# A gated layer on one core: the values pass placed ahead of the pass of seven products, with the weight sums stored in between

## The chip, the cores and the metric

The kernel runs on one core of one Trainium2 chip. The metric is device time in microseconds (us) of one execution; the runs of a kernel are given as a median with the lowest and highest.

## What is computed

The reference is one layer of a hybrid encoder on x (4096 positions, 1024 features): RMS norm, one input projection, then three groups side by side (dilated attention, a gating unit, attention into 256 memory tokens), each times SiLU of its gate, one output projection, a residual and a last RMS norm. The change touches the gating unit alone:

```python
uv = jax.nn.gelu(sg_uv)
u, vv = jnp.split(uv, 2, axis=-1)
vv = layer_norm(vv, sg_ln_g[layer], sg_ln_b[layer])
vv = vv.reshape(B, S // SG_CHUNK, SG_CHUNK, N_SG_GROUPS, SG_GROUP_DIM)
mixed = jnp.einsum('gpq,bcqge->bcpge', sg_w[layer], vv)
mixed = mixed + jnp.transpose(sg_b[layer])[None, None, :, :, None]
y_sg = (u * mixed.reshape(B, S, SG_WIDTH)) * jax.nn.silu(g_sg)
```

sg_uv and g_sg are 1024 and 512 columns of h @ w_in. So three blocks of 512 columns are projected for it: u, vv and the gate.

## The kernel before

All matmuls work on pairs of numbers: every operand is split into a high part (ACT copies it to fp32r, tiles xh, wh) and a low part (VectorE subtracts the high part, tiles xl, wl), and each product is three matmuls (high x high, high x low, low x high). A 128x512 block with 1024 input features is 8 x 3 = 24 matmuls.

The work runs in passes. **Pass A** (lines 242 to 318) projects q, k and the attention's values over eight tiles T of 512 positions. **Pass U** (lines 393 to 467) computes u and the gate together: as a 2x2 block product with seven instead of eight sub-products (Winograd's form). For that, split_parts (lines 338 to 391) forms seven weight blocks B11, T2, B22, T1, T3, B21, T4 of four 128x512 tiles each, in three rounds at the last T of pass A; it reads 40 raw blocks of 256 KB. Pass U has 16 rounds r of 256 positions. prep(r) loads x (line 404), scales it on POOL (line 406), forms the sums S1 to S4 on POOL (lines 418, 419, 422, 426) and splits seven x blocks (lines 414, 415). A round is seven product() calls of 12 matmuls (line 434) into three accumulators b1, b2, b3, with additions by VectorE in between (lines 447 to 460), and GELU and SiLU on ACT (lines 461 to 464); the result GELU(u) * SiLU(gate) is stored to DRAM as ug (line 467). **Pass B** (lines 470 to 525), the values pass, projects vv with Wvv over eight T, four blocks j each; GELU (line 498), layer norm (lines 500 to 506) and a split (lines 507, 508) follow on ACT, VectorE and POOL; then 24 matmuls of 128x256 (line 520, tile pm) form the weight sums, and VectorE adds the bias and multiplies by u, which was loaded back from ug (lines 492, 524). **Pass C** starts with the memory tokens: projections with Wmv (line 595) and Wmk (line 608), rsb (line 331), weights Wqm (line 587).

Buffers that all passes share lie in pool px: five raw tiles, ten xh and ten xl. Weight tiles lie in slots 0 (px), 1, 2 (pool pw) and 3 (pool pz); slots 0 to 2 hold eight tiles each, so a weight takes the slot when the one before is used up. Inside a pass every pass has its own pool, which lies over that of the pass before it.

The order of the instructions on each engine is made by a planner, which goes by its own estimates of cost and takes what is ready, earlier lines first. From the last T of pass B to line 616 in pass C the order on TensorE, ACT and VectorE is that of the program (ORDERED, line 52). The order of the passes is in build:

```python
with tc.tile_pool(name="pz", bufs=2, reuse_waits="tile") as b.pz:
    b.pass_a()
    b.pass_u()
b.order = ExitStack()
b.pass_b()
gates = b.pass_g(env)
for _ in b.pass_c(env):
    next(gates)
```

Of the kernel before, what the change touches and what calls it, by code (L numbers as in the profile page):

```python
# [18 lines left out]
S = 4096  # L19
# [35 lines left out]
class Builder:  # L55
    def __init__(self, ctx, tc, a):
# [38 lines left out]
        dt("ug", [S, 512])  # L95
# [146 lines left out]
    def pass_a(self):  # L242
        nc, tc, a = self.nc, self.tc, self.a
        with tc.tile_pool(name="pa", bufs=2, reuse_waits="tile") as p, \
# [26 lines left out]
            for T in range(NT):  # L271
# [23 lines left out]
                if T == NT - 1:  # L295
                    values(T, X, rs)
                    self.split_parts(0)
                for W, done, dh, dl in ((Wq, pq, self.qH, self.qL), (Wk, pk, self.kH, self.kL)):
                    for cb in range(4):
# [5 lines left out]
                        if T == NT - 1 and cb == 3:  # L305
                            self.split_parts(1 if W is Wq else 2)
# [28 lines left out]

    PAIR = 2048, 3072

    def split_parts(self, rnd):


        nc = self.nc
        if rnd == 0:
            self.WS = {}
        g_ = self.g_in

        def raw(i, j, kt):
            t = self.px.tile([P, 512], F32, name="raw", tag="raw", bufs=5)
            nc.sync.dma_start(t, self.a["w_in"][(4 * i + kt) * P:(4 * i + kt + 1) * P, self.PAIR[j]:self.PAIR[j] + 512])
            return t

        def put(name, slot, src, g, kt):
            pool = (self.px, self.pw, self.pw, self.pz)[slot]
            n = 4 if slot == 3 else 8
            h = pool.tile([P, 512], F32R, name="wh", tag="wh%d" % slot, bufs=n)
            lo = pool.tile([P, 512], F32R, name="wl", tag="wl%d" % slot, bufs=n)
            self.WS[name, kt] = h, lo
            if g is None:
                nc.scalar.copy(h, src)
                nc.vector.tensor_sub(lo, src, f(h))
            else:  # L360
                nc.scalar.activation(h, src, AF.Copy, scale=g)
                nc.vector.scalar_tensor_tensor(lo, src, g, f(h), ALU.mult, ALU.subtract)

        def tmp():
            return self.pz.tile([P, 512], F32, name="wt", tag="wt", bufs=2)

        for kt in range(4):
            g1, g2 = g_[:, kt:kt + 1], g_[:, kt + 4:kt + 5]
            b11, b12, b22 = raw(0, 0, kt), raw(0, 1, kt), raw(1, 1, kt)
            if rnd == 0:  # L370
                put("B11", 0, b11, g1, kt)
            if rnd != 1:
                d, t2 = tmp(), tmp()
                nc.gpsimd.tensor_sub(d, b12, b11)
                nc.scalar.activation(d, d, AF.Copy, scale=g1)
                nc.vector.scalar_tensor_tensor(t2, b22, g2, d, ALU.mult, ALU.subtract)
            if rnd == 0:
                put("T2", 0, t2, None, kt)
                put("B22", 3, b22, g2, kt)
            elif rnd == 1:  # L380
                d, t3 = tmp(), tmp()
                nc.gpsimd.tensor_sub(d, b12, b11)
                put("T1", 1, d, g1, kt)
                nc.scalar.activation(b12, b12, AF.Copy, scale=g1)
                nc.vector.scalar_tensor_tensor(t3, b22, g2, b12, ALU.mult, ALU.subtract)
                put("T3", 1, t3, None, kt)
            else:
                b21 = raw(1, 0, kt)
                put("B21", 2, b21, g2, kt)
                nc.vector.scalar_tensor_tensor(t2, b21, g2, t2, ALU.mult, ALU.subtract)  # L390
                put("T4", 2, t2, None, kt)

    def pass_u(self):

        nc, tc, a = self.nc, self.tc, self.a
        with tc.tile_pool(name="pu", bufs=1, reuse_waits="tile") as p, tc.tile_pool(name="ppu", bufs=2, space=PSUM, reuse_waits="tile") as pp:
            rsb = {}

# [1037 lines left out]
```

## Time and profile before

| what | value |
|---|---|
| median of 3 runs | 3135.18 us (3132.35 to 3145.68) |
| the profiled execution's own time | 3133.94 us |
| its span, first to last instruction | 3132.2 us |
| mean granted TensorE clock | 0.983 of full speed |
| TensorE busy | 2985.4 us, 95% |
| first and last store of ug (pass U's rounds) | 643.9 and 934.5 us |

Times in the rows count from the start of the span. PE is TensorE's matmuls, PEld its weight loads, DVE is VectorE, POOL is GpSimd, SPq the queue of DMA issues of SyncE. The granted clock is 1.00 at 2.4 GHz and 0.50 at 1.2 GHz; a value in between is a mean over the stretch. An arrow in brackets names what ended the idle time ahead of an instruction. A matmul's given length overlaps with the next one's.

### The profile page before, as it was taken

Reading aid. Unit: us, or ns where it says so; the run is one execution under the profiler, and the core shown is the slowest. Engines: PE = TensorE matmul, PEld = TensorE weight load, DVE = VectorE, ACT = ScalarE, POOL = GpSimd, SP = SyncE. Lnnn points to the kernel's source line nnn. Section 1 sums busy time; section 2 is a strip of 40 time slices with the busy share of each in tenths; the row PEclk is TensorE's granted clock in tenths of the full one; section 3 lists DMA queues with packets and bytes.
Section 4 is the critical chain, followed back from the end, with each engine's and each line's share of the span. In section 5 each row is a group of like instructions: output and inputs, shape, how many; then the busy total and the mean of one; then the engine's idle time right before and its main releaser. Section 6 shows DMA issues by size and latency. Waiting matters only on the chain. (4 is left out here: it accounts for less than half of the span.)

```text
span 3132.2 us, 44554 instructions
## 1 busy us (share of the span) xinstructions
PE 2985.4 (95%) x15658; PEld 2496.4 (80%) x15658; DVE 1626.9 (52%) x3889; ACT 1343.0 (43%) x2675; POOL 555.6 (18%) x800
## 2 busy tenths in 40 slices
PE   9989999599999989999999989999999998999999
PEld 7777888478887878888888868888888876888887
DVE  4222323676657776555553335656665564443443
ACT  5213112345553446555553346677767652111111
POOL 1102113465511100000000011222212211121120
PEclk9999999799999999999999999999999999999999
DMA  8558545522235553112117557777877468777773
GB/s 285 185 162 255 174 135 171 192 88 88 88 109 172 174 177 113 48 55 73 48 53 218 167 126 153 150 150 161 164 162 152 105 174 225 212 192 203 208 190 100
DMA packets 373895, 474.43 MB, mean 151 GB/s; under 512 B 155331, under 2 KB 247838, under 8 KB 364454
## 3 DMA queue, kind: packets, MB, share of 16 engines
q1 hardware_dynamic: 355656, 429.20, 49.3%
q0 software_dynamic: 17440, 41.33, 5.3%
q8 instruction: 124, 2.03, 0.3%
q10 hardware_dynamic: 576, 1.05, 0.1%
q14 instruction: 99, 0.81, 0.1%
HBM read 332.83 MB, written 138.60 MB: 151 GB/s over the span
## 5 line engine op out<-in xcount | busy, mean ns | idle before, releaser
L201 PE MATMUL acc<-xl,wh 128*128 128x512 f32 x1192 | 470.9, 395 | 13.3 <-DVE xl L187 13.2
L200 PE MATMUL acc<-xh,wh 128*128 128x512 f32 x1192 | 472.4, 397 | 8.1 <-ACT xh L186 8.1
L202 PE MATMUL acc<-xh,wl 128*128 128x512 f32 x1192 | 470.5, 395 | 0.0
L880 ACT ACTIVATE p<-ring,negm 128x256 f32<-128x256 f32 (+1 forms) x768 | 330.7, 478 | 167.5 <-DVE negm L867 167.5
L791 DVE CUSTOM_DVE_ANT_0 ring<-s,tab 128x256 f32<-128x256 f32 (+1 forms) x768 | 272.1, 392 | 109.9 <-PE s L786 87.6
L201 PEld LDWEIGHTS acc<-xl,wh 128*128 128x128 f32 x1192 | 226.0, 190 | 66.1 <-DVE xl L187 17.8
L200 PEld LDWEIGHTS acc<-xh,wh 128*128 128x128 f32 x1192 | 225.8, 189 | 59.6 <-ACT xh L186 10.3
L202 PEld LDWEIGHTS acc<-xh,wl 128*128 128x128 f32 x1192 | 226.4, 190 | 47.3
L933 PE MATMUL o<-ph,vt 128*65 128x256 f32 (+1 forms) x1280 | 246.5, 340 | 9.3 <-DMA vt<-v 9.3
L949 DVE COPY oacc<-o 65x512 f32<-65x512 f32 x192 | 132.1, 688 | 203.2 <-PE o L933 140.7
L786 PE MATMUL s<-khh,qs 128*128 128x256 f32 (+1 forms) x768 | 228.4, 322 | 0.0
L186 ACT CAST xh<-raw 128x512 fp32r<-128x512 f32 x256 | 151.7, 620 | 172.1 <-DMA raw<-in_xT_s 96.6
L933 PEld LDWEIGHTS o<-ph,vt 128*65 128x65 f32 x1280 | 166.9, 140 | 70.8 <-issue 11.9
L434 PE MATMUL b<-wh,xh 128*128 128x512 f32 x448 | 178.2, 398 | 34.8 <-ACT xh L414 27.8
L187 DVE TENSOR_TENSOR xl<-raw,xh 128x512 fp32r<-128x512 f32 x256 | 167.7, 686 | 79.3 <-ACT xh L186 77.8
L1257 PE MATMUL acc<-w,aa 128*128 128x512 f32 x768 | 191.4, 399 | 15.3 <-ACT aa L1242 9.9
L200 PE MATMUL acc<-wh,xh 128*128 128x512 f32 x512 | 199.7, 390 | 0.0
L202 PE MATMUL acc<-wh,xl 128*128 128x512 f32 x512 | 199.6, 390 | 0.0
L201 PE MATMUL acc<-wl,xh 128*128 128x512 f32 x512 | 199.5, 390 | 0.0
L786 PE MATMUL s<-kll,qs 128*128 128x256 f32 (+1 forms) x768 | 198.8, 283 | 0.0
L1257 PEld LDWEIGHTS acc<-w,aa 128*128 128x128 f32 x768 | 146.0, 191 | 50.4 <-ACT aa L1242 10.4
L434 PE MATMUL b<-wh,xl 128*128 128x512 f32 x448 | 177.6, 396 | 3.4 <-DVE xl L415 3.4
(277 smaller groups left out, 5817.3 us busy)
## 6 DMA issues: line engine op xcount, KB each, us to landing
raw<-in_xT_s SPq DMA_DIRECT2D x256, 256.0 KB
raw<-in_w_in SPq DMA_DIRECT2D x96, 256.0 KB
og<-oD SPq DMA_DIRECT2D x16, 1536.0 KB
w3k<-wD SPq DMA_DIRECT2D x32, 768.0 KB
oD<-oacc POOLq DMA_DIRECT2D x46, 512.0 KB, 4.7
xn<-in_x_s SPq DMA_DIRECT2D x32, 512.0 KB
v<-t POOLq DMA_DIRECT2D x128, 128.0 KB, 5.5
xr<-in_xT_s SPq DMA_DIRECT2D x16, 1024.0 KB
```

The costliest lines, as they stand in the source:

```text
L186: nc.scalar.copy(h[:, :n], raw[:, :n])
L187: nc.vector.tensor_sub(lo[:, :n], raw[:, :n], f(h[:, :n]))
L200: nc.tensor.matmul(out, lh, rh, start=i == 0, stop=False)
L201: nc.tensor.matmul(out, lh, rl, start=False, stop=False)
L202: nc.tensor.matmul(out, ll, rh, start=False, stop=i == n - 1)
L434: nc.tensor.matmul(ps, l[:, k, :], w, start=first and k + i == 0, stop=k == 3 and i == 2, skip_group_check=True)
L786: nc.tensor.matmul(ps[:, b1, :B["n"]], q, kv, start=i == 0, stop=i == 1)
L791: self.last_dve = nc.vector.tensor_tensor_reduce(out=ring[:, bi, :n], in0=ps[:, b1, :n], in1=e["tab"][:, c, 64 * B["o"]:64 * B["o"] + n], ...
L880: nc.scalar.activation(out, in_, AF.Exp, bias=e["negm"][:, bi:bi + 1], scale=1.0)
L933: nc.tensor.matmul(o[:, o0:o1], vt[:, t, :], pT[:, c0:c1], start=t == 0, stop=t == 4, skip_group_check=True)
L949: nc.vector.tensor_copy(dst, o)
L1257: nc.tensor.matmul(ps, l, w, start=a, stop=o, skip_group_check=True)
```

## The change

The passes run in the order A, B, U, C. Pass B stores the weight sums with their bias, in a DRAM tensor mix, and pass U multiplies by them. In detail: (1) split_parts is gone; at the last T of pass A, Wvv is loaded into slot 0. (2) Pass B's function mix evicts the sums with ACT (Identity with a bias) instead of VectorE and stores y; it is called after the first projection of the next T, and for the last T after the loop. (3) split_early forms B11, T1, T2, T3, B22 at T = 2 to 5 of pass B (slots 1, 2, 3), 12 raw blocks; split_late forms B21 and T4 (slot 0) after the last projection of pass B, 16 raw blocks. w_block and put_w, not shown, are raw and put of split_parts. (4) split_x replaces prep; for round 0 it is called inside pass B and uses four raw tiles; sums are formed in place; the scaling is in two halves. (5) A round of pass U also loads 256 rows of mix (y) and multiplies them on POOL. (6) The stretch in program order begins with the last round of pass U, and the loads of the memory tokens, Wmv and Wmk move there. pass_u's product() is the same as before and is left out.

```diff
-        dt("ug", [S, 512])
+        dt("mix", [S, 512])
...
-                    self.split_parts(0)
+                    self.Wvv = self.load_w(0, self.w_in(2560), self.g_in)
...
-                        if T == NT - 1 and cb == 3:
-                            self.split_parts(1 if W is Wq else 2)
...
-            raw = p.tile([P, 8, P], F32, name="sgraw")
+            raw = p.tile([P, 8, P], F32, name="sgraw", tag="y")
...
+            def mix(T, vvh, vvl):
+                y = p.tile([P, 4, 512], F32, name="y", tag="y")
+                for g2 in range(4):
+                    pm = pp.tile([P, 2, 256], F32, name="pm", bufs=4)
+                    for g in (2 * g2, 2 * g2 + 1):
+                        cs = slice(g * 64, (g + 1) * 64)
+                        self.mm3(pm[:, g % 2, :], [((sw[0][:, g, :], sw[1][:, g, :]), (vvh[:, :, cs], vvl[:, :, cs]))])
+                    for g in (2 * g2, 2 * g2 + 1):
+                        cs = slice(g * 64, (g + 1) * 64)
+                        pv = pm[:, g % 2, :].rearrange("p (c e) -> p c e", e=64)
+                        nc.scalar.activation(y[:, :, cs], pv, AF.Identity, bias=sgb[:, g:g + 1])
+                nc.sync.dma_start(self.mix[T * TT:(T + 1) * TT, :].rearrange("(j p) c -> p j c", p=P), y)
+            vv = None
             for T in range(NT):
-                if T == NT - 1:
-                    self.order.enter_context(tc.manual_schedule(engines=ORDERED))
                 X = self.load_x(a["xT_s"][:, T * TT:(T + 1) * TT])
-                vvh = p.tile([P, 4, 512], F32R, name="vvh")
-                vvl = p.tile([P, 4, 512], F32R, name="vvl")
-                u = p.tile([P, 4, 512], F32, name="u", tag="u", bufs=2)
-                nc.sync.dma_start(u, self.ug[T * TT:(T + 1) * TT, :].rearrange("(j p) c -> p j c", p=P))
                 for j in range(4):
                     rs = rsn[:, 4 * T + j:4 * T + j + 1]
-                    t = p.tile([P, 512], F32, name="t", tag="t1", bufs=3)
+                    self.proj_N(ps, self.Wvv, X, j)
+                    if j == 0:
+                        if T > 0:
+                            mix(T - 1, *vv)
+                        vv = [p.tile([P, 4, 512], F32R, name=n) for n in ("vvh", "vvl")]
+                    if j == 3 and T == NT - 1:
+                        X = self.split_x(0, None)
+                        for kt in range(4):
+                            self.split_late(kt)
+                    t = p.tile([P, 512], F32, name="t", tag="t1", bufs=2)
...
+                    nc.scalar.copy(vv[0][:, j, :], t)
+                    nc.vector.tensor_sub(vv[1][:, j, :], t, f(vv[0][:, j, :]))
+                if 2 <= T < 6:
+                    self.split_early(T - 2)
+            mix(NT - 1, *vv)
+            self.X0 = X
...
+    def split_early(self, kt):
+        nc = self.nc
+        if kt == 0:
+            self.WS = {}
+        g1, g2 = self.g_in[:, kt:kt + 1], self.g_in[:, kt + 4:kt + 5]
+        b11, b12, b22 = self.w_block(0, 0, kt), self.w_block(0, 1, kt), self.w_block(1, 1, kt)
+        self.put_w("B11", 1, b11, g1, kt)
+        nc.gpsimd.tensor_sub(b11, b12, b11)
+        self.put_w("T1", 2, b11, g1, kt)
+        nc.scalar.activation(b11, b11, AF.Copy, scale=g1)
+        nc.vector.scalar_tensor_tensor(b11, b22, g2, b11, ALU.mult, ALU.subtract)
+        self.put_w("T2", 1, b11, None, kt)
+        nc.scalar.activation(b12, b12, AF.Copy, scale=g1)
+        nc.vector.scalar_tensor_tensor(b12, b22, g2, b12, ALU.mult, ALU.subtract)
+        self.put_w("T3", 2, b12, None, kt)
+        self.put_w("B22", 3, b22, g2, kt)
+    def split_late(self, kt):
+        nc = self.nc
+        g1, g2 = self.g_in[:, kt:kt + 1], self.g_in[:, kt + 4:kt + 5]
+        b21, b11, b12, b22 = self.w_block(1, 0, kt), self.w_block(0, 0, kt), self.w_block(0, 1, kt), self.w_block(1, 1, kt)
+        self.put_w("B21", 0, b21, g2, kt)
+        nc.gpsimd.tensor_sub(b11, b12, b11)
+        nc.scalar.activation(b11, b11, AF.Copy, scale=g1)
+        nc.vector.scalar_tensor_tensor(b11, b22, g2, b11, ALU.mult, ALU.subtract)
+        nc.vector.scalar_tensor_tensor(b11, b21, g2, b11, ALU.mult, ALU.subtract)
+        self.put_w("T4", 0, b11, None, kt)
+    def split_x(self, r, p):
+        nc, a = self.nc, self.a
+        if r % 2 == 0:
+            self.rsb = self.pz.tile([P, TT], F32, name="rsb", bufs=1)
+            nc.sync.dma_start(self.rsb, self.rD[:, r * NI:r * NI + TT].broadcast_to([P, TT]))
+        rs = self.rsb[:, r % 2 * NI:(r % 2 + 1) * NI].rearrange("p (o t) -> p o t", o=1)
+        src = a["xT_s"][:, r * NI:(r + 1) * NI].rearrange("(k p) t -> p k t", p=P)
+        if p is None:
+            x = [self.px.tile([P, 512], F32, name="raw", tag="raw", bufs=5).rearrange("p (k t) -> p k t", k=2) for _ in range(4)]
+            for i in range(4):
+                nc.sync.dma_start(x[i], src[:, 2 * i:2 * i + 2])
+            A = [[x[2 * j + e][:, :, P * i:P * (i + 1)] for e in range(2)] for i in range(2) for j in range(2)]
+        else:
+            t = p.tile([P, KT, NI], F32, name="xr", bufs=2)
+            nc.sync.dma_start(t, src)
+            x = [t[:, :4], t[:, 4:]]
+            A = [[t[:, 4 * j:4 * j + 4, P * i:P * (i + 1)]] for i in range(2) for j in range(2)]
+        for t in x:
+            nc.gpsimd.tensor_mul(t, t, rs.broadcast_to([P, t.shape[1], NI]))
+        a11, a12, a21, a22 = A
+        n = len(a11)
+        s1 = self.px.tile([P, 512], F32, name="raw", tag="raw", bufs=5).rearrange("p (k t) -> p k t", k=4)
+        s1 = [s1[:, 4 // n * e:4 // n * (e + 1)] for e in range(n)]
+        B = {}
+        def put(name, srcs):
+            h = self.px.tile([P, TT], F32R, name="xh", tag="xh", bufs=10).rearrange("p (k t) -> p k t", k=4)
+            lo = self.px.tile([P, TT], F32R, name="xl", tag="xl", bufs=10).rearrange("p (k t) -> p k t", k=4)
+            for e, s in enumerate(srcs):
+                ks = slice(4 // n * e, 4 // n * (e + 1))
+                nc.scalar.copy(h[:, ks], s)
+                nc.vector.tensor_sub(lo[:, ks], s, f(h[:, ks]))
+            B[name] = h, lo
+        def gp(op, out, x, y):
+            for o, i, k in zip(out, x, y):
+                op(o, i, k)
+        put("A11", a11)
+        gp(nc.gpsimd.tensor_add, s1, a21, a22)
+        gp(nc.gpsimd.tensor_sub, a21, a11, a21)
+        gp(nc.gpsimd.tensor_sub, a11, s1, a11)
+        put("S2", a11)
+        put("S1", s1)
+        put("S3", a21)
+        put("A12", a12)
+        gp(nc.gpsimd.tensor_sub, a12, a12, a11)
+        put("A22", a22)
+        put("S4", a12)
+        return B
...
+            X = self.X0
+            for r in range(2 * NT):
+                last = r == 2 * NT - 1
+                if last:
+                    self.order.enter_context(tc.manual_schedule(engines=ORDERED))
+                b1, b2, b3 = [pp.tile([P, 512], F32, name="b%d" % i, bufs=2) for i in range(3)]
+                p1, u2, u3 = [p.tile([P, 512], F32, name=n) for n in ("p1", "u2", "u3")]
+                w, y = [p.tile([P, 2, 512], F32, name=n, bufs=2) for n in "wy"]
+                rows = slice(r * NI, (r + 1) * NI)
+                nc.sync.dma_start(y, self.mix[rows, :].rearrange("(j p) c -> p j c", p=P))
+                product(b1, "A11", "B11", True)
+                nc.scalar.copy(p1, b1)
+                product(b2, "S2", "T2", True)
+                nc.vector.tensor_add(u2, b2, p1)
+                if last:
                     self.mem = self.load_mem(0) + self.load_mem(1)
-                    self.Wmk = self.load_w(0, a["w_kv"][:, :512], self.g_mem)
-                if T == NT - 2:
+                product(b3, "S1", "T1", True)
+                product(b2, "S3", "T3", False)
+                nc.vector.tensor_add(u3, b2, p1)
+                if last:
                     self.Wmv = self.load_w(1, a["w_kv"][:, 512:1024], self.g_mem)
-                if T == NT - 1:
+                product(b1, "A12", "B21", False)
+                nc.vector.tensor_add(u3, b3, u3)
+                product(b2, "A22", "T4", False)
+                product(b3, "S4", "B22", False)
+                if not last:
+                    X = self.split_x(r + 1, p)
+                else:
                     self.mem += self.load_mem(2) + self.load_mem(3)
...
-                nc.sync.dma_start(self.ysg[T * TT:(T + 1) * TT, :].rearrange("(j p) c -> p j c", p=P), u)
+                nc.vector.tensor_add(w[:, 1], b2, p1)
+                nc.vector.tensor_add(u2, b3, u2)
+                nc.scalar.activation(w[:, 0], b1, AF.Gelu_apprx_tanh)
+                nc.scalar.activation(w[:, 1], w[:, 1], AF.Gelu_apprx_tanh)
+                nc.scalar.activation(u3, u3, AF.Silu)
+                nc.scalar.activation(u2, u2, AF.Silu)
+                nc.gpsimd.tensor_mul(w, w, y)
+                nc.vector.tensor_mul(w[:, 0], w[:, 0], u2)
+                nc.vector.tensor_mul(w[:, 1], w[:, 1], u3)
+                nc.sync.dma_start(self.ysg[rows, :].rearrange("(j p) c -> p j c", p=P), w)
+            self.Wmk = self.load_w(0, a["w_kv"][:, :512], self.g_mem)
...
+                b.pass_a()
+                b.order = ExitStack()
                 with tc.tile_pool(name="pz", bufs=2, reuse_waits="tile") as b.pz:
-                    b.pass_a()
+                    b.pass_b()
                     b.pass_u()
-                b.order = ExitStack()
-                b.pass_b()
                 gates = b.pass_g(env)
                 for _ in b.pass_c(env):
                     next(gates)
```

## Rows read from the trace of the kernel before

**Rows 1.** The page's busy times and shares of the span, all engines.

```profile
PE 2985.4 (95%) x15658; PEld 2496.4 (80%) x15658; DVE 1626.9 (52%) x3889; ACT 1343.0 (43%) x2675; POOL 555.6 (18%) x800
```

**Rows 2.** Stretches: length; PE, PEld, DVE, ACT, POOL busy; granted clock; DMA share; GB/s.

```profile
480.00:576.00 96.00, 95.96 (x425) 78.94 (x424) 46.69 (x62) 29.36 (x47) 33.19 (x42) 1.00 0.63 198
576.00:604.00 28.00, 0.28 (x1) 0.28 (x2) 12.75 (x18) 7.15 (x12) 8.03 (x4) 0.57 0.80 260
604.00:647.00 43.00, 32.56 (x124) 24.88 (x125) 38.07 (x27) 17.65 (x28) 35.24 (x18) 0.88 0.23 74
647.00:930.00 283.00, 283.00 (x1222) 228.91 (x1221) 185.44 (x211) 146.02 (x211) 125.74 (x62) 1.00 0.27 88
740.00:780.00 40.00, 40.00 (x175) 32.40 (x174) 27.11 (x30) 20.54 (x31) 21.72 (x11) 1.00 0.27 86
930.00:1134.00 204.00, 196.26 (x938) 163.31 (x936) 155.80 (x311) 79.81 (x131) 35.58 (x31) 1.00 0.52 172
1138.00:1144.00 6.00, 5.81 (x29) 5.52 (x30) 4.78 (x8) 4.25 (x7) 0.00 (x0) 0.58 0.50 160
1144.00:1162.00 18.00, 11.39 (x51) 8.90 (x49) 12.21 (x22) 9.32 (x14) 0.00 (x0) 0.95 0.78 254
1162.00:1180.00 18.00, 17.90 (x113) 16.86 (x114) 13.19 (x23) 11.13 (x19) 0.00 (x0) 0.86 0.75 233
```

**Rows 3.** TensorE's waits, 480 to 1220: total us, times, longest us.

```profile
PE b L434 <- ACT xh L414: 27.8, 1, 27.8
PE pm L200 <- ACT vvh L507: 11.8, 8, 4.5
PE b L434 <- DVE u L447: 7.0, 2, 6.2
PE acc L608 <- ACT rsb L331: 6.6, 1, 6.6
PE b L434 <- DVE xl L415: 3.4, 1, 3.4
```

**Rows 4.** Timeline of TensorE, weight sums: start, length, instruction, idle before, releaser.

```profile
985.34 0.73 PE L200 MATMUL pm<-vvh,sgwh 128*128 128x256 f32 x4 [1.02 <-ACT vvh L507]
...
1138.04 0.58 PE L200 MATMUL pm<-vvh,sgwh 128*128 128x256 f32 x1 [4.47 <-ACT vvh L507]
```

**Rows 5.** Timeline of SyncE's queue, POOL and ACT at the first turn.

```profile
589.22 1.12 SPq L404 DMA_DIRECT2D xr<-in_xT_s  x2
...
598.52 4.49 POOL L406 TENSOR_TENSOR xr<-xr,rsb 128x2048 f32<-128x2048 f32 x1 [11.18 <-DMA xr<-in_xT_s]
...
603.05 0.62 ACT L414 CAST xh<-xr 128x512 fp32r<-128x512 f32 x1 [10.47 <-POOL xr L406]
```

**Rows 6.** Groups by line: shapes, count, busy us, mean ns, idle before.

```profile
L558 ACT ACTIVATE pr<-s,mx 128x256 f32<-128x256 f32 x128 | 58.9, 474 | 0.4
...
L1233 POOL TENSOR_TENSOR og<-og 128x1024 f32<-128x1024 f32 x16 | 38.5, 2403 | 101.2 <-DVE og L1231 101.2
...
L524 DVE SCALAR_TENSOR_TENSOR u<-pm,sgb,u 128x256 f32<-128x256 f32 x64 | 25.8, 477 | 1.6 <-PE pm L202 0.9
...
L913 ACT COPY pq<-pt 128x256 f32<-128x256 f32 x64 | 22.4, 349 | 0.0
...
L461 ACT ACT_TABLE_LOAD x16 | 20.5, 1283 | 0.3
```

**Rows 7.** Line 390: durations in ns, first and last start.

```profile
L390 DVE SCALAR_TENSOR_TENSOR wt<-raw,g_in,wt x4: 746/752/1753, 571.5 to 591.1; 128x512 f32<-128x512 f32 x4
```

**Rows 8.** Line 467, the store at a round's end: first and last start.

```profile
L467 SPq DMA_DIRECT2D ug<-w x16: 359/360/378, 643.9 to 934.5; - x16
```

**Rows 9.** Timeline of POOL and VectorE inside a steady product round.

```profile
770.31 4.61 POOL L406 TENSOR_TENSOR xr<-xr,rsb 128x2048 f32<-128x2048 f32 x1 [1.31 <-DMA xr<-in_xT_s]
...
772.48 3.00 DVE L415 TENSOR_TENSOR xl<-s,xh 128x512 fp32r<-128x512 f32 x1
...
776.60 0.68 DVE L415 TENSOR_TENSOR xl<-s,xh 128x512 fp32r<-128x512 f32 x1
```

More of the change, by code (lines that the diff above doesn't have):

```diff
@@ L332, in bcast @@
         return rsb
[L336 to L391, printed above, removed]
@@ L506, in pass_b @@
                     nc.vector.scalar_tensor_tensor(t, t, rv, lnb, ALU.mult, ALU.add)
-                    nc.scalar.copy(vvh[:, j, :], t)
-                    nc.vector.tensor_sub(vvl[:, j, :], t, f(vvh[:, j, :]))
-                if T == NT - 1:
+                    nc.scalar.copy(vv[0][:, j, :], t)
[4 more added lines that the diff above has]
+            self.X0 = X
@@ new lines, with w_block, put_w @@
+    PAIR = 2048, 3072
+    def w_block(self, i, j, kt):
+        t = self.px.tile([P, 512], F32, name="raw", tag="raw", bufs=5)
+        self.nc.sync.dma_start(t, self.a["w_in"][(4 * i + kt) * P:(4 * i + kt + 1) * P, self.PAIR[j]:self.PAIR[j] + 512])
+        return t
+    def put_w(self, name, slot, src, g, kt):
+        nc = self.nc
+        pool = (self.px, self.pw, self.pw, self.pz)[slot]
+        n = 4 if slot == 3 else 8
+        h = pool.tile([P, 512], F32R, name="wh", tag="wh%d" % slot, bufs=n)
+        lo = pool.tile([P, 512], F32R, name="wl", tag="wl%d" % slot, bufs=n)
+        self.WS[name, kt] = h, lo
+        if g is None:
+            nc.scalar.copy(h, src)
+            nc.vector.tensor_sub(lo, src, f(h))
+        else:
+            nc.scalar.activation(h, src, AF.Copy, scale=g)
+            nc.vector.scalar_tensor_tensor(lo, src, g, f(h), ALU.mult, ALU.subtract)
@@ new lines, in split_late @@
+    def split_late(self, kt):
+        nc = self.nc
+        g1, g2 = self.g_in[:, kt:kt + 1], self.g_in[:, kt + 4:kt + 5]
[6 more added lines that the diff above has]
+        self.put_w("T4", 0, b11, None, kt)
@@ new lines, in pass_u, with product @@
+    def pass_u(self):
+        nc, tc, a = self.nc, self.tc, self.a
+        with tc.tile_pool(name="pu", bufs=1, reuse_waits="tile") as p, tc.tile_pool(name="ppu", bufs=2, space=PSUM, reuse_waits="tile") as pp:
+            def product(ps, xn, wn, first):
+                for k in range(4):
+                    (xh, xl), (wh, wl) = X[xn], self.WS[wn, k]
+                    for i, (l, w) in enumerate(((xh, wh), (xh, wl), (xl, wh))):
+                        nc.tensor.matmul(ps, l[:, k, :], w, start=first and k + i == 0, stop=k == 3 and i == 2, skip_group_check=True)
+            X = self.X0
[13 more added lines that the diff above has]
+                if last:
@@ L516, in pass_b @@
-                for g2 in range(4):
-                    pm = pp.tile([P, 2, 256], F32, name="pm", bufs=4)
-                    for g in (2 * g2, 2 * g2 + 1):
-                        cs = slice(g * 64, (g + 1) * 64)
-                        self.mm3(pm[:, g % 2, :], [((sw[0][:, g, :], sw[1][:, g, :]), (vvh[:, :, cs], vvl[:, :, cs]))])
-                    for g in (2 * g2, 2 * g2 + 1):
-                        cs = slice(g * 64, (g + 1) * 64)
-                        pv = pm[:, g % 2, :].rearrange("p (c e) -> p c e", e=64)
-                        nc.vector.scalar_tensor_tensor(u[:, :, cs], pv, sgb[:, g:g + 1], u[:, :, cs], ALU.add, ALU.mult)
```

74 lines of the change are left out of this document (1 added, 73 removed).

## The prediction

> **What bounds the kernel now.** I read the page's busy times first, then a table of the stages around the change, then TensorE's waits in that stretch, then the single rows on both sides of each wait. TensorE is busy 95% of the span [rows 1]. The change adds and removes no matmul, so it can only win or lose what TensorE idles, or runs at a low clock, between 480 and 1220 us. The stage table [rows 2] shows four places. At the end of pass A and in the steady rounds of the seven products (480:576, 647:930) TensorE is busy throughout at full clock. Between lies the turn from pass A to the products: 28 us with one matmul record, then 43 us with 32.6 us busy and a clock of 0.88. The values pass has 7.7 us of idle in 204, and the turn into pass C again has waits and a lowered clock. The waits [rows 3] name them: 27.8 us once for an x tile, 7.0 and 3.4 us in the first product rounds, 11.8 us in eight waits of the weight sums, 6.6 us once at line 608.
>
> What 65 us are lost is made of: the idle time of the first turn is 27.8 + 7.0 + 3.4 = 38.2 us. Its slow clock: 283 us hold 1222 matmul records, 0.232 each, so 124 records need 28.7 us and took 32.6, 3.8 us lost. Together 42. The weight sums wait 11.8 us, of which 4.5 us are the last one [rows 4], 7.3 us the other seven. After the last one 6 us pass at a clock of 0.58, 6 x 0.42 = 2.5 us lost; after line 608 the loss is 18 x 0.14 = 2.5 us. So 42 + 7.3 + 4.5 + 2.5 + 6.6 + 2.5 = 65 us: more than the change can give.
>
> **The first turn goes.** In the kernel before, the first x of the products (line 404) is issued at 589.2, behind the 40 weight blocks of split_parts in the same queue. POOL starts to scale it at 598.5, 11.2 us after its last work, takes 4.5 us, and ACT's first cast comes at 603.1 [rows 5]; TensorE starts 0.6 us later. In the change pass A is followed by an ordinary x load and a projection with Wvv, whose eight blocks are loaded behind the last values block, under eight projections of pass A. The same turnover of x tiles happens at every T of pass A and of the values pass, and TensorE never waits there for an x tile: its waits are those of products, weight sums and line 608 [rows 3]. I take 1 us; bounds 0 and 4 (new constants and pool space). The constants of the weight sums have four projections to arrive, so they cost nothing; without that cover it would be their one load.
>
> **The interior of the values pass.** Today each weight sum starts 1.0 us too late [rows 4]: two matmuls of the projection ahead of it come behind it. Now it stands behind a whole projection, so 2 x 0.23 = 0.5 us of each wait is covered. VectorE loses 56 evictions of 0.477 us (line 524) there, and ACT gets them as Identity with bias, which no row shows: between 0.349 and 0.474 us for the same shape, 22 to 30 us in all; if each group also cost two table loads of 1.283 us it would be 20 us more [rows 6]. ACT is busy 80 of 204 us [rows 2], so the low value is free and even the high one fits. At T = 2 to 5 split_early adds 3 loads, 7 ACT, 7 VectorE and 1 POOL instructions each, some 5 us of VectorE per 26 us; with line 524 gone VectorE stays near three quarters busy. But the chain that ends in vvh stands in the same queues, so some links wait for a 0.75 us operation. I take 4 us for seven waits; bounds 2 and 10. The x loads behind split_early share its five raw buffers, and have a whole T to get through: nothing.
>
> **The new turn, values to products.** It is the open term. The first x is split through raw buffers ahead of the last projection, and B11, T1, T2, T3, B22 are ready; two of ten x buffers are free, the rest follow as that projection consumes its tiles. So TensorE has the first four products (48 matmuls, 11 us) under the last vvh chain, which took at least 4.5 us behind its projection [rows 4]: that wait goes. Late are B21 and T4: their slot is Wvv's, so they can only be written while the last projection runs, and each of four steps needs four of the five raw buffers through a chain of load, POOL, ACT, VectorE twice, ACT, VectorE. The nearest row is the same chain in split_parts: line 390 starts at 571.5 and, three steps later, at 591.1, 6.5 us a step [rows 7]. If the first T4 is ready 6 us after the last projection ends, the last is ready at 6 + 3 x 6.5 = 25.5. TensorE wants it after the weight sums (2.8), five products (13.9) and nine matmuls (2.1), at 18.8. The gap is 7 us; I take 9 with the slow clock behind it. Below it is 0 (the planner can fill it with the next round's first products); above, with nothing beside it, 30. VectorE is also crowded in the first two rounds, as it was before (7.0 + 3.4 us); with the first x already split I take 4 of those 10, bounds 0 and 14.
>
> **The steady rounds.** One round takes (934.5 - 643.9) / 15 = 19.4 us [rows 8]. Each round keeps its matmuls, its seven splits and its drains; POOL's scaling comes in two halves, and POOL gets the product with the stored mix, 128x1024, 2.40 us [rows 6]. SP's transfers change places: 16 loads of y and 8 stores of mix for 8 loads of u and 16 stores of ug, the same bytes. POOL is busy 21.7 of 40 us [rows 2], 10.5 a round, so 12.9 of 19.4 after. TensorE wants the next x a full round later. I take 0, with a rival for it below.
>
> **The turn into pass C.** The last weight sum no longer stands there, so its 4.5 + 2.5 us go. Line 608 waits for rsb, which is behind the weight casts on ACT; there are now sixteen such blocks in front of it (Wmk and Wqm), eight of them loadable only when T4's slot is free. The products' last drains also stand on ACT, in an order that is now fixed from the last round on: Wmv's casts between the products come before the last GELU, which nobody on TensorE waits for, and Wmv itself, whose slot B11 and T2 free after two products, has five products (14 us) to load eight blocks under; without that cover some of them would be waited for. I keep 9.5 us for 9.1; bounds 5 and 14.
>
> **The sum.** Left over: 1 + 4 + 9 + 4 + 0 + 9.5 = 27.5 of 65 us. The gain is 37.5 us against the profiled execution's own 3133.9 (a span of 3132.2), so 3096 us; the median of the three runs shown is 1.2 us above that execution. The bounds of all terms together give a gain of 65 - 7 = 58 to a loss of 7, which no one chance supports; with the new turn between 0 and 25 us and the others near their values the likeliest case reaches from 3080 to 3120.
>
> **Rivals.** First, POOL and VectorE get in each other's way: the rounds become longer, and the kernel slower. In the trace a split that takes 0.68 us took 3.00 us when it started under POOL's 4.61 us scaling, and ended 0.56 us after it [rows 9]. The Trainium skill's page "SBUF — State Buffer", section "SBUF: two separate sides", says why: GpSimd and VectorE operations with two SBUF inputs take turns at one pair of ports, locked for the whole instruction. The trace agrees. As a mechanism of this kernel: nine VectorE operations a round read two SBUF tiles, 9 x 0.69 = 6.2 us; with POOL's 12.9 that is 19.1 of 19.4 us, against 16.7 now. By this sum alone the rounds just fit, so the forecast keeps 0. It decides once more than 0.3 us a round goes in hand-overs, and for additions that stand behind a blocked split. If all of VectorE's work takes turns with POOL (five PSUM reads of 0.69 more), 22.5 us are needed, 3.1 more for 15 rounds, 47 us: 3143. Against it: TensorE is a round behind the split, and halves block for less long. Chance 0.12.
>
> Second, the late weights cost all of the 30 us, with a crowded VectorE behind them (14): the stall has moved. 3096 + 21 + 10 = 3127. For it: four chain steps of 6.5 us and one set of five buffers. Against it: 14 us of matmuls beside them. Chance 0.14.
>
> Third, the change doesn't do what it says: the gap of the first turn stays, because the new pools wait for pass A's last stores as the old ones did, or the planner puts the weight work in front of the first x. Then some 25 us stay: 3121. The ready path of px speaks against it. Chance 0.08.
>
> **Chances.** The forecast has 0.66. A measurement of this kernel can tell some 0.5%, 16 us, from no change. Of the forecast's cases nearly all are faster by more; the second and third rival lie on both sides of 3119, the first is within 0.5% or above 3151. So 0.72 faster, 0.20 the same, 0.08 slower. The range from 3078 to 3132 holds the forecast's own range and the second and third rival's prices.
>
> **What would show it.** Right: no TensorE gap above 4 us between pass A and the values pass; vvh waits of about half a microsecond; one gap of 5 to 10 us at the products with B21 or T4 in the first round, released by VectorE or ACT; rounds of 19.4 us. Wrong: rounds above 20 us with long splits (first rival); a gap above 20 us at the first T4 (second), or ahead of the values pass (third).

## The result, and the profile after

The changed kernel takes 3207.9 us (median of 4, 3205.4 to 3211.1) against 3135.0 for the kernel before (median of 4, 3132.4 to 3145.7): 1.0226 times as long, 95% interval 1.0201 to 1.0252. The prediction said 3096 us, and its range ended at 3132. The profiled execution took 3211.1 us, with a span of 3209.3.

The page's busy times answer to [rows 1]. TensorE is busy 30.6 us longer with the same 15658 matmuls, and idle 46.5 us more (193.3 of 3209.3 against 146.8 of 3132.2):

```profile
PE 3016.0 (94%) x15658; PEld 2511.1 (78%) x15658; DVE 1574.1 (49%) x3832; ACT 1361.9 (42%) x2745; POOL 599.2 (19%) x834
```

The table of stretches (columns as in [rows 2]): pass A into the values pass, its middle, its end, the first product rounds, the other rounds, the turn into pass C.

```profile
576.00:616.00 40.00, 36.89 (x164) 30.45 (x163) 27.51 (x50) 18.93 (x33) 5.51 (x5) 0.96 0.51 165
616.00:748.00 132.00, 123.54 (x587) 101.59 (x586) 101.24 (x183) 78.25 (x146) 30.78 (x23) 1.00 0.45 144
748.00:815.00 67.00, 51.52 (x242) 44.12 (x242) 41.37 (x75) 28.58 (x62) 23.89 (x22) 0.87 0.28 88
815.00:857.00 42.00, 29.17 (x117) 22.48 (x115) 25.42 (x25) 17.58 (x28) 24.20 (x14) 0.93 0.53 171
857.00:1180.00 323.00, 279.37 (x1096) 221.18 (x1097) 154.36 (x189) 126.13 (x187) 175.01 (x93) 0.91 0.29 94
1180.00:1236.00 56.00, 44.88 (x185) 35.71 (x184) 29.08 (x44) 29.86 (x43) 4.76 (x2) 0.92 0.45 143
```

The first turn is gone: TensorE is busy 36.9 of the 40 us behind pass A, where it had lost 28. But the product rounds, which ran at full clock without a gap [rows 2], now idle 44 of 323 us at a clock of 0.91. TensorE's waits from 480 to 1320 us (columns as in [rows 3]) name what it waits for, the first addition to u2 in a round (line 520):

```profile
PE b L505 <- DVE u L520: 55.3, 14, 8.4
PE pm L200 <- ACT vvh L385: 26.8, 8, 8.5
PE acc L629 <- ACT rsb L329: 6.9, 1, 6.9
PE b L505 <- DVE u L529: 4.2, 1, 4.2
PE b L505 <- DVE xl L478: 1.2, 1, 1.2
```

The store at a round's end answers to [rows 8]:

```profile
L545 SPq DMA_DIRECT2D ysg<-w x16: 359/359/378, 857.1 to 1219.7; - x16
```

(1219.7 - 857.1) / 15 = 24.2 us a round, 4.8 more than before. Fifteen times 4.8 is 72 us: the slowdown is the length of the rounds. The rest cancels: from 576 us to the first matmul that waits for rsb (1161.9 us before, 1235.3 now), what lies outside these fifteen rounds took 295.3 us before and takes 296.7 now. TensorE waits 8.9 us less there: the waits of the first turn (27.8, 3.4 and 6.2 us [rows 3]) are gone, and 15 us more at the weight sums (26.8 against 11.8) and 13 us in the first two rounds have come. But it is busy 10.4 us longer, with more matmuls outside the rounds (1143 records against 1109) and a clock of 0.87 from 748 to 815 us.

**One round, in order of time.** These are rows picked from the timeline of all engines, between two waits of TensorE (start, length, engine, instruction, idle before it and what released it):

```profile
1035.95 0.77 PE L505 MATMUL b<-wh,xh 128*128 128x512 f32 x1 [3.21 <-DVE u L520]
...
1046.66 0.63 ACT L539 ACTIVATE w<-w 128x512 f32<-128x512 f32 x1 [0.22 <-DVE w L536]
1047.43 2.39 POOL L465 TENSOR_TENSOR xr<-xr,rsb 128x1024 f32<-128x1024 f32 x1 [1.65 <-DMA xr<-in_xT_s]
1049.78 2.38 POOL L542 TENSOR_TENSOR w<-w,y 128x1024 f32<-128x1024 f32 x1
1052.13 2.38 POOL L465 TENSOR_TENSOR xr<-xr,rsb 128x1024 f32<-128x1024 f32 x1
1052.20 2.86 DVE L544 TENSOR_TENSOR w<-w,u 128x512 f32<-128x512 f32 x1 [4.97 <-POOL w L542]
1054.98 0.68 DVE L537 TENSOR_TENSOR u<-b,u 128x512 f32<-128x512 f32 x1
1055.74 1.28 ACT L541 ACT_TABLE_LOAD   x1 [6.62 <-DVE u L537]
1057.03 0.63 ACT L541 ACTIVATE u<-u 128x512 f32<-128x512 f32 x1
1057.69 0.74 DVE L543 TENSOR_TENSOR w<-w,u 128x512 f32<-128x512 f32 x1 [0.94 <-ACT u L541]
1058.68 0.69 DVE L478 TENSOR_TENSOR xl<-xr,xh 128x512 fp32r<-128x512 f32 x1 [0.25 <-ACT xh L477]
1059.29 0.68 DVE L520 TENSOR_TENSOR u<-b,p 128x512 f32<-128x512 f32 x1
1060.12 0.77 PE L505 MATMUL b<-wh,xh 128*128 128x512 f32 x1 [3.02 <-DVE u L520]
```

GELU of w is done at 1047.3. GpSimd first scales half of the next x, then multiplies w by mix. VectorE's product with u3 (line 544) stands idle for that 4.97 us, then takes 2.86 us in place of 0.7, since GpSimd scales the second half beside it. Behind it, in VectorE's queue, stands an addition that needs nothing of all this (line 537); behind that Silu u2, the last product, and the next round's first addition, for which TensorE waits.

Near the end no next x is left to scale. The same instructions there, again picked from the timeline:

```profile
1169.69 2.39 POOL L542 TENSOR_TENSOR w<-w,y 128x1024 f32<-128x1024 f32 x1 [1.59 <-ACT w L539]
1172.11 0.69 DVE L544 TENSOR_TENSOR w<-w,u 128x512 f32<-128x512 f32 x1 [2.56 <-POOL w L542]
1175.44 0.69 DVE L543 TENSOR_TENSOR w<-w,u 128x512 f32<-128x512 f32 x1 [1.44 <-ACT u L541]
1177.04 0.68 DVE L520 TENSOR_TENSOR u<-b,p 128x512 f32<-128x512 f32 x1
```

VectorE still waits for GpSimd's product, but its own product takes 0.69 us, TensorE has no wait for this line 520, and the store of this round comes 19.7 us after the one before it; the next comes 19.5 us later. So the product's 2.4 us alone fit into a round; together with the scaling ahead of it and behind it they do not.

### The profile page after: what moved, and what is told of

Read it like the earlier page. It is cut to its first block, busy times and chain, and to the rows that moved or that the text cites. A ratio compares the mean times of both kernels' runs of the same rounds, so it can differ in the third digit from the quotient of the medians.

```text
span 3209.3 us, 44651 instructions
## 1 busy us (share of the span) xinstructions
PE 3016.0 (94%) x15658; PEld 2511.1 (78%) x15658; DVE 1574.1 (49%) x3832; ACT 1361.9 (42%) x2745; POOL 599.2 (19%) x834
## 5 line engine op out<-in xcount | busy, mean ns | idle before, releaser
L505 PE MATMUL b<-wh,xh 128*128 128x512 f32 x448 | 188.4, 421 | 59.5 <-DVE u L520 55.3
L954 PEld LDWEIGHTS o<-ph,vt 128*65 128x65 f32 x1280 | 166.0, 139 | 74.7 <-issue 15.5
L505 PE MATMUL b<-wh,xl 128*128 128x512 f32 x448 | 186.3, 416 | 1.2 <-DVE xl L478 1.2
L505 PE MATMUL b<-wl,xh 128*128 128x512 f32 x448 | 186.6, 416 | 0.0
```

What stands on the lines that cost most here:

```text
L505: nc.tensor.matmul(ps, l[:, k, :], w, start=first and k + i == 0, stop=k == 3 and i == 2, skip_group_check=True)
L954: nc.tensor.matmul(o[:, o0:o1], vt[:, t, :], pT[:, c0:c1], start=t == 0, stop=t == 4, skip_group_check=True)
```

## The experiments

Two theories. **Chain**: GpSimd's product is a link ahead of VectorE's last products, and the next round's first addition stands behind these. **Capacity**: GpSimd and VectorE, which hold each other up, have too much work for 19.4 us, wherever the product stands. Then the waits outside the rounds. All edits are to the changed kernel unless said otherwise. "Round" is the mean distance of the stores in the middle rounds, after the first few (of the changed kernel, 936 to 1157 us: 24.5).

| run | edit | us | ratio to before (95%) | round, us |
|---|---|---|---|---|
| changed kernel | | 3207.9 | 1.0226 (1.0201, 1.0252) | 24.5 |
| e1_order | u2 += b3 ahead of the last products | 3199.8 | 1.0192 (1.0175, 1.0209) | 23.8 |
| e3_no_mix | no product with mix | 3142.6 | 1.0012 (0.9999, 1.0025) | 19.5 |
| e4_swap | GpSimd multiplies early operands | 3158.4 | 1.0061 (1.0044, 1.0078) | 20.6 |
| e7_swap_order | e4 with e1 | 3158.1 | 1.0057 (1.0037, 1.0077) | 20.6 |
| e10_hold | last products held into the next round | 3151.2 | 1.0049 (1.0028, 1.0069) | 20.7 |
| e6_vector_order | e1, VectorE multiplies by mix | 3158.9 | 1.0065 (1.0044, 1.0086) | 20.9 |
| e5_before_load | before, idle GpSimd products | 3166.0 | 1.0093 (1.0075, 1.0111) | 19.5 |
| e13_before_x | before, GpSimd products that read x | 3158.0 | 1.0050 (1.0035, 1.0066) | 20.5 |
| e8_first_x | first x on VectorE, later | 3194.4 | 1.0173 (1.0146, 1.0201) | 24.4 |
| e9_mix2 | weight sums two projections later | 3176.8 | 1.0121 (1.0094, 1.0148) | 24.2 |
| e11_all | e10 (behind the second addition to u3), e8 and e9 | 3120.1 | 0.9943 (0.9925, 0.9962) | 20.1 |
| e12_all_vector | e6, e8 and e9 | 3131.7 | 0.9984 (0.9973, 0.9994) | 20.9 |

### Is it the product with mix?

```diff
-                nc.gpsimd.tensor_mul(w, w, y)
```

> Leaves out the product with the mixed values (its load stays). Both theories expect the rounds of the kernel before, 19.4 us, and 3208 - 15 x 4.8 = 3136 us. If the load of the mixed values or the new split of x is the cause, the rounds stay near 24 us and the time near 3207 us.

It came as expected: rounds of 19.5 us and a time 0.1% from the kernel before. The new split of x in halves and the loads of mix cost the rounds nothing.

### The order on VectorE alone

```diff
-                nc.vector.tensor_add(u2, b3, u2)
+                late = nc.vector.tensor_add(u2, b3, u2)
...
-                nc.vector.tensor_mul(w[:, 0], w[:, 0], u2)
-                nc.vector.tensor_mul(w[:, 1], w[:, 1], u3)
+                self.after(nc.vector.tensor_mul(w[:, 0], w[:, 0], u2), late)
+                self.after(nc.vector.tensor_mul(w[:, 1], w[:, 1], u3), late)
```

> Only the order on VectorE differs from the changed kernel: both products with w stand behind the addition u2 += b3; the same instructions, the same loads of GpSimd and VectorE. Chain theory (the addition stands behind a product that waits for GpSimd's product with mix, so Silu u2, the last product and the next round's u2 come late): the addition starts some 5 us earlier; the last product is then still held by GpSimd's product (ended 1052.2 us in the round read) and by the scaling of the second half of x (to 1054.5), so that the next u2 comes near 1056 in place of 1059.3: 3.3 us a round off 24.2, rounds near 21 us, time near 3208 - 15 x 3.3 = 3158 us. Capacity theory (VectorE and GpSimd hold each other's SBUF port so long that 19.4 us of round don't hold both): rounds stay near 24 us and the time near 3207 us.

A miss for the chain theory's number: 3199.8 us. VectorE's timeline of a round shows why:

```profile
1046.99 0.69 DVE L537 TENSOR_TENSOR u<-b,u 128x512 f32<-128x512 f32 x1 [1.51 <-PE b L505]
1050.23 2.86 DVE L544 TENSOR_TENSOR w<-w,u 128x512 f32<-128x512 f32 x1 [2.55 <-POOL w L542]
1053.02 1.77 DVE L478 TENSOR_TENSOR xl<-raw,xh 128x512 fp32r<-128x512 f32 x1
1054.72 1.76 DVE L543 TENSOR_TENSOR w<-w,u 128x512 f32<-128x512 f32 x1
1056.40 0.68 DVE L478 TENSOR_TENSOR xl<-xr,xh 128x512 fp32r<-128x512 f32 x1
1057.00 0.68 DVE L520 TENSOR_TENSOR u<-b,p 128x512 f32<-128x512 f32 x1
```

The addition did come early. But both products still stand behind GpSimd's, and the next round's addition behind both, with a split of x that GpSimd's next work slows to 1.77 us. It was not the one displaced addition; it is the whole tail behind GpSimd's product.

### Holding the tail back

The tail goes behind the next round's first addition; no engine gets more or less to do.

```diff
+            def finish(prev, w, u2, u3, rows):
+                self.after(nc.vector.tensor_mul(w[:, 0], w[:, 0], u2), prev)
+                self.after(nc.vector.tensor_mul(w[:, 1], w[:, 1], u3), prev)
+                nc.sync.dma_start(self.ysg[rows, :].rearrange("(j p) c -> p j c", p=P), w)
...
-                p1, u2, u3 = [p.tile([P, 512], F32, name=n) for n in ("p1", "u2", "u3")]
+                p1 = p.tile([P, 512], F32, name="p1")
+                u2, u3 = [p.tile([P, 512], F32, name=n, bufs=2) for n in ("u2", "u3")]
...
-                nc.vector.tensor_add(u2, b2, p1)
+                first = nc.vector.tensor_add(u2, b2, p1)
+                if r > 0:
+                    finish(first, *held)
...
-                nc.vector.tensor_mul(w[:, 0], w[:, 0], u2)
-                nc.vector.tensor_mul(w[:, 1], w[:, 1], u3)
-                nc.sync.dma_start(self.ysg[rows, :].rearrange("(j p) c -> p j c", p=P), w)
+                held = w, u2, u3, rows
+            finish(None, *held)
```

> The changed kernel with the two last products of a round (w times u2, w times u3) and its store held back until VectorE has done the first addition of the next round, with two tiles each for u2 and u3; GpSimd's product with mix, and every engine's work, stay as they are. Chain theory: nothing that TensorE waits for stands behind GpSimd's product any more, rounds go from 24.2 to 19.4 to 20 us and the time to 3208 - 15 x 4.5 = 3140 us. Capacity theory: the same instructions and ports, rounds stay near 24 us and the time near 3207 us.

3151.2 us, rounds of 20.7. Capacity would have left 24. TensorE's waits from 918 to 1104 us in this kernel, and a stretch of four of its rounds, then four rounds of the changed kernel (columns as in [rows 2]):

```profile
PE b L505 <- DVE u L533: 8.1, 9, 1.2
```

```profile
918.46:1000.91 82.45, 78.95 (x337) 62.38 (x336) 66.64 (x57) 37.83 (x56) 56.77 (x29) 1.00 0.34 109
```

```profile
963.10:1060.20 97.10, 84.94 (x337) 67.16 (x337) 46.81 (x57) 37.88 (x56) 53.07 (x28) 0.93 0.28 93
```

Line 533 is here the first addition to u3, which now stands behind the held products. The same 337 matmuls take 82.4 us here and 97.1 there. The 14.7 us are 8.7 of idle time (12.2 against 3.5) and 6.0 of longer matmuls at a lower clock: each wait of 3 us costs half as much again behind it. VectorE is busier in the faster kernel: its splits now run where they are slowed by GpSimd (1.21 us in the mean of 55, against 0.69), and TensorE waits for none of them.

### The product on operands that are early

```diff
-                nc.gpsimd.tensor_mul(w, w, y)
-                nc.vector.tensor_mul(w[:, 0], w[:, 0], u2)
-                nc.vector.tensor_mul(w[:, 1], w[:, 1], u3)
+                nc.gpsimd.tensor_mul(y[:, 1], y[:, 1], u3)
+                nc.gpsimd.tensor_mul(y[:, 0], y[:, 0], w[:, 0])
+                nc.vector.tensor_mul(y[:, 1], y[:, 1], w[:, 1])
+                nc.vector.tensor_mul(y[:, 0], y[:, 0], u2)
```

(and the store takes y). With the additions ordered as in e1 it is e7.

> GpSimd still does the product with the mixed values, 1024 elements a partition and round, but on operands that are ready early (mix times Silu u3, mix times Gelu of b1, as two products of 512), and VectorE multiplies the rest and the store takes the tile of mix. Chain theory: no engine's queue stands behind GpSimd's product when b2 and b3 end; rounds of 19.4 to 20.5 us and 3135 to 3155 us. Capacity theory: GpSimd's busy time is the same, rounds stay near 24 us, 3207 us.

> The kernel with GpSimd's product on early operands (3158 us, 20.56 us a round), and u2 += b3 put ahead of VectorE's product of y and w, which took 2.88 us of GpSimd's port time there. Chain theory: the 0.8 us of wait a round go; rounds near 19.5 us, 3158 - 15 x 1 = 3143 us. If the products stand in the way wherever they are, rounds stay at 20.5 us and the time at 3158 us.

Taking the product out of the chain in another way gives the same round, 20.6 us. In e7 the order gave nothing (20.6 again): TensorE still waits 0.8 us for line 520 in every round. So 1.1 us a round are left, which putting this addition first did not touch.

### GpSimd's work without the chain

In the kernel before, twice. First products on a scratch tile alone (`nc.gpsimd.tensor_mul(z, z, z)`, four of 256 elements a round); then the same number reading the scaled x:

```diff
                 put("S4", s4)
+                for j in range(4):
+                    nc.gpsimd.tensor_mul(z, x[:, j, :], x[:, j + 4, :])
```

> The kernel before, with GpSimd products of 4 x 256 elements on a scratch tile in every round of products, that nothing waits for. Chain theory: rounds 19.4 us, 3135 us, up to 20 us a round where scaling comes late. Capacity theory: rounds near 24 us, 3207 us.

> The kernel before with 4 products of 256 elements a partition on GpSimd in every round, read from the scaled x and written to a scratch tile (2.4 us a round, as much as the product with mix), that no engine waits for. The earlier run with a scratch tile alone had no such products in its steady rounds: they had run ahead of time. Chain theory: rounds stay within 0.6 us of 19.4, time 3135 to 3145 us. Capacity theory: rounds near 24 us, 3207 us.

The first failed as a test: with nothing to wait for, the products ran ahead of their rounds, the first 20 of them (15.5 us) in front of the first x's scaling. The wait of 27.8 us [rows 3] became 35.1, and the steady rounds, left without them, took 19.5 us. The second has them in every round, here GpSimd's group from 740 to 900 us and TensorE's waits from 694 to 901:

```profile
L430 POOL TENSOR_TENSOR z<-xr 128x256 f32<-128x256 f32 x32 | 32.0, 999 | 2.5
```

```profile
PE b L437 <- DVE u L450: 7.4, 9, 1.4
```

4.0 us more GpSimd time a round, for which nobody waits, lengthen the round from 19.4 to 20.5 us, 1.1 us. So crowding is real, outside the 0.6 us that I had allowed, and far from 4.8. It is the size of what e4, e7 and e10 had left; that theirs is the same thing is not shown, and in e10 about half of it was order again (e11, below).

### VectorE in place of GpSimd

```diff
-                nc.gpsimd.tensor_mul(w, w, y)
+                nc.vector.tensor_mul(w, w, y)
```

(with the order of e1).

> The product with mix is done by VectorE in place of GpSimd, and u2 += b3 stands ahead of the products with u. Chain theory: no wait for GpSimd is left in that queue, rounds of 19.4 to 20 us, 3208 - 15 x 4.5 = 3140 us. Rival (VectorE itself is the limit of these rounds: 1.3 us more on it, beside locks of 5 us a round): rounds of 21 us or more, 3160 us or more.

Rounds of 20.9 us, nearly the rival's 21: with GpSimd out of it, each round still waits 1.1 us for line 520. Its 3158.9 us are no better than e4's.

### The waits outside the rounds

ScalarE's and GpSimd's rows ahead of the seventh weight sum in the changed kernel, and TensorE's at the seventh and eighth:

```profile
776.14 3.63 POOL L483 TENSOR_TENSOR raw<-raw 128x256 f32<-128x256 f32 x5
...
778.25 0.40 ACT L477 CAST xh<-raw 128x256 fp32r<-128x256 f32 x1 [7.09 <-POOL raw L483]
778.56 0.61 ACT L385 CAST vvh<-t 128x512 fp32r<-128x512 f32 x1
...
779.23 1.22 PE L200 MATMUL pm<-vvh,sgwh 128*128 128x256 f32 x4 [6.97 <-ACT vvh L385]
808.91 1.01 PE L200 MATMUL pm<-vvh,sgwh 128*128 128x256 f32 x3 [8.51 <-ACT vvh L385]
```

The last cast of the values stands in ScalarE's queue behind a cast of the first x, which waits 7.09 us for GpSimd. The edits: `nc.vector` for `nc.gpsimd` where that first x is scaled and combined, with the block of `split_x(0, None)` and `split_late` issued at the end of the last projection's turn (e8); the projections 0 and 1 of a tile both issued ahead of the mix of the tile before (e9).

> The changed kernel with the first x of the product pass scaled and combined on VectorE in place of GpSimd, and issued behind the last normalisation of the values pass. Theory (the casts of that x stand in ScalarE's queue in front of the last values casts and wait there for GpSimd: waits for the seventh and eighth mix of 7.0 and 8.5 us): the waits fall to 2 to 3 us each, 3208 - 10 = 3198 us. Rival (the last weights and x are late anyway; the time moves into the first two rounds): 3207 us.

> The changed kernel with the mix of a tile issued two projections into the next one, in place of one. Theory (the values of the last quarter come 1.8 us after one projection of 5.3 us): the waits of 1.8 us at mixes 2 to 5 and of 3.1 and 1.1 us go and that of 7.0 us falls to 2, 3208 - 15 = 3193 us; the eighth, which has no projection behind it, stays at 8.5 us. Rival (the first values of the next tile then wait for the mix to give the tile back, and the wait returns one projection later): 3207 us.

From the values pass's first statistics (line 378) to the last weight sum the changed kernel takes 220.1 us, e8 212.7, e9 197.7. In e8 the seventh wait falls from 7.0 to 1.1 us and the eighth from 8.5 to 5.9. In e9 the first six are gone and the seventh is 1.6; the eighth stays at 8.4. Both rivals fall. e9 gained more than its 16.8 us of waits: the changed kernel's clock was 0.87 from 748 to 815 us, around the seventh and eighth wait, and one of the two is now short.

### All together

> The held products (3151 us; here behind the second addition to u3, which the held pair delayed by 0.9 us a round), the first x on VectorE and issued late (-13 us), and the mix two projections later (-31 us) together, GpSimd's product as in the changed kernel. If the three causes are separate: 3151 - 13 - 31 - 13 = 3094 us. If one hides behind another: above 3110 us.

> As the run before it, but with the product with mix on VectorE and u2 += b3 ahead of the last products, in place of held products. If the three causes are separate and VectorE has room: 3208 - 65 - 13 - 31 = 3099 us; if VectorE is the limit of the rounds, 3120 us or more.

e11 beats both kernels: 3120.1 us, 0.57% below the kernel before (interval 0.38 to 0.75%). The sum of 3094 was 26 us too good, past the 3110 at which one cause was to hide behind another; most of the 26 us is the size of the terms. Against e10 the values pass (first statistics to eighth weight sum) is 26.6 us shorter, 193.2 against 219.8; my two terms said 44. They were differences of whole times, each uncertain by some 8 us, where the profiles show the values pass 7.4 us shorter in e8 and 22.4 in e9, and the two overlap in the seventh wait, which each takes away. From the eighth weight sum to pass C e11 takes 366.6 us, 7.3 less than e10 and 59.8 less than the changed kernel; I had put 13, but the rounds went to 20.1 us, not to 19.8, and only from 20.7. With the held products behind the second addition to u3, TensorE's wait for these additions fell from 0.9 to 0.4 us a round. e12 keeps VectorE's rounds of 20.9 us and ends 0.16% below before, where its rival (VectorE as the limit) had put it.

## Why the prediction was wrong

**The step that failed is "The steady rounds: I take 0".** It counted GpSimd's busy time (12.9 of 19.4 us) and found room. It never asked what stands behind the added instruction. Its line "TensorE wants the next x a full round later" is true of x; the operand that became late is u2, whose single tile the last product must free before the next round's first addition can write it. In the kernel before none of the additions, activations and products from b2 and b3 to that point reads a result of GpSimd's; the change put in 2.4 us of product, up to 2.4 of scaling ahead of it, and a VectorE product that 2.4 more of scaling slows down. The term should have been 4.8 us a round: in the four rounds from 963 us 3.0 of wait each, and 1.8 of matmuls at a lowered clock. The rounds near the end, of 19.7 and 19.5 us, show that the product by itself would have cost nothing: it is the chain with x's scaling in the same queue that the sum left out. No run put the product ahead of the scaling in GpSimd's queue.

**The first rival named the sign, not the mechanism.** Its crowding exists: e13 shows 1.1 us a round, 17 us in all, against the 3.1 us at most that the rival priced. The Trainium skill's page "SBUF — State Buffer", section "SBUF: two separate sides", which the rival drew on, says that the two engines take turns at one pair of ports; the trace agrees, with line 544 taking 2.69 us in the mean of 13 rounds, and 0.69 where GpSimd has no scaling beside it. But the sign that the prediction gave for this rival, long splits, did not show: in nine rounds from 936 us 54 of the 63 splits took 0.69 us in the mean, and the long operation was line 544. And three quarters of the loss are a queue's order, which e10 takes away without removing any of the work. Its time, 3143, also kept the forecast's gains in the values pass, which did not come.

**The first turn: right.** There is no wait between pass A and the values pass, and none for the constants.

**The interior of the values pass: wrong.** I took 4 us, bounds 2 and 10, for seven waits; they are 18.3. Up to the sixth the waits are 1.1 to 3.1 us, where [rows 4] show 1.0. Here is one chain of the last quarter, GELU to cast, in the changed kernel:

```profile
714.35 0.68 ACT L376 ACTIVATE t<-acc,rs_x 128x512 f32<-128x512 f32 x1
...
717.49 1.79 POOL L423 TENSOR_TENSOR raw<-raw 128x512 f32<-128x512 f32 x1 [4.59 <-DMA raw<-in_xT_s]
...
719.24 0.99 POOL L110 TENSOR_TENSOR rv<-rsq_t,mhalf 128x1 f32<-128x1 f32 x1
720.27 0.75 DVE L384 SCALAR_TENSOR_TENSOR t<-t,rv,lnb 128x512 f32<-128x512 f32 x1 [0.44 <-POOL rv L110]
...
721.06 0.61 ACT L385 CAST vvh<-t 128x512 fp32r<-128x512 f32 x1
```

From GELU to cast it is 6.7 us; in the kernel before, at the weight sum of 1062.8 us, 5.0. The weight split's subtraction on GpSimd (line 423) stands ahead of the power for the normalisation (line 110). It does so ahead of all four waits of 1.8 us and not ahead of the sixth, of 1.1; no run moved it. I had seen that links would wait "for a 0.75 us operation" and priced no operation of GpSimd's. The seventh wait, 7.0 us, is the first x: its split ahead of the last projection was put in at no cost, and on ScalarE's queue its casts stood ahead of the values' last cast.

**The new turn: place and cause wrong.** The wait stands at the eighth weight sum, ahead of the products, and TensorE never waited for B21 or T4. They were late: the last T4 tile was done at 832.5 us, 32 us after the last projection's end (800.4), where the prediction had 25.5. But TensorE had waited 8.5 us for the eighth weight sum and 4.7 for the first addition to u2 by then; what these weights would cost without those waits no run shows. GpSimd's and ScalarE's rows ahead of the eighth weight sum:

```profile
805.49 1.42 POOL L439 TENSOR_TENSOR raw<-raw 128x512 f32<-128x512 f32 x1 [3.32 <-DMA raw<-in_w_in]
806.87 0.54 POOL L110 TENSOR_TENSOR rv<-rsq_t,mhalf 128x1 f32<-128x1 f32 x1
```

```profile
806.94 0.72 ACT L440 ACTIVATE raw<-raw,g_in 128x512 f32<-128x512 f32 x1 [3.75 <-POOL raw L439]
808.24 0.62 ACT L385 CAST vvh<-t 128x512 fp32r<-128x512 f32 x1 [0.57 <-DVE t L384]
```

The last values' power on GpSimd stands behind the first late weight's subtraction, which waits for its load; the prediction's "that wait goes" is wrong, and the wait is longer than the 4.5 us in the same place before [rows 4]. No run moved the late weights alone, so their share of the 8.5 us stays open; with the first x on VectorE and issued later (e8), 5.9 us of it stay.

**The crowded first two rounds: the size wrong.** I took 4 us, bounds 0 and 14; the waits there are 4.7, 1.2 and 8.0 us, 13.8 together. Behind the first stands this row of ScalarE:

```profile
825.94 0.58 ACT L518 COPY p<-b 128x512 f32<-128x512 f32 x1 [3.04 <-DMA mix<-y]
```

The first write to p1 waits for the store of the last weight sums, since the rounds' pool lies over that of the values pass. That is the mechanism of the third rival, at the new turn in place of the first. The prices of the second and third rival, 3127 and 3121, both lie above 3119, not on both sides of it as the prediction says.

**The turn into pass C: right**, 4.2 + 6.9 = 11.1 us of waits against 9.5, inside 5 to 14.

## What to carry to other kernels

Before moving an operation to an idle engine, follow its result: which instruction of an in-order queue waits for it, what stands behind that instruction, and who needs that; an engine two thirds busy can still be the link that sets the round. Where a late consumer is the trouble, give its operand a second buffer and issue the consumer behind the next round's critical step; that gave back three quarters of the loss here without removing any work. Giving the moved operation operands that are ready early (e4) gave back as much with no second buffer. And test a load on an engine with products that read the round's own data, or they will run at another time.

## What the runs showed of the hardware

A wait of 3 us in every round cost more than itself: in the four rounds shown TensorE's clock was 0.93 in the mean, and 6.0 us of the 14.7 lost lie in the matmuls behind the waits. In e10, with waits of 0.6 to 1.2 us a round, it stayed at 1.00 in the four rounds shown; so it did in the changed kernel's values pass from 616 to 748 us, with waits of 1.8 us some 27 us apart. What decides between these no run here tells apart.

GpSimd's operations were slowed too. An operation of line 483 on 128x512 took 1.66 us at 1158.70 us, beside two splits on VectorE (1157.94 to 1159.22), and 1.30 us at 1178.47, where VectorE did nothing beside it.
